# Which engine computes the low halves of two weight units behind the output projection

## The chip, the cores and the metric

The kernel runs on one core of one Trainium2 chip. The metric is the device time of one launch in microseconds (us), the median of several runs. Five engines work side by side, each through its own queue in order: TensorE (PE in the profile, PEld for its weight loads), VectorE (DVE), ScalarE (ACT), GpSimd (POOL) and SyncE (SP), which here only issues transfers.

## What is computed

The reference is one step of a two-layer decoder trunk, run for a prompt of 512 tokens and for 64 sample tokens (8 sequences of 8) with the same weights. One layer, cut to what matters here:

```python
h    = x * (1 + sc1) + sh1
proj = h @ w_in                                  # 22 blocks of 128 columns
mix  = concat([retention(proj), sliding_window(proj)]) @ w_out      # 8 blocks
x    = layer_norm(ALPHA * x + g1 * mix, ln1_g, ln1_b)
h2   = x * (1 + sc2) + sh2
up   = h2 @ w_up                                 # 44 blocks
f    = silu(conv3(up)_a) * conv3(up)_b
x    = layer_norm(ALPHA * x + g2 * (f @ w_down), ln2_g, ln2_b)      # 22 units
```

## The kernel before, in words

Everything lies transposed: 128 features on the partitions, 576 tokens along a row, so `x` is eight tiles of 128x576. Tokens are worked on in two halves of 288 (`HA`).

**Weights.** All weights come as a stream of units of 128x1024 f32, 96 for a layer (`UNITS`): 22 for `w_in`, 8 for `w_out`, 44 for `w_up`, 22 for `w_down`, in order of use. `Weights` (lines 72 to 113) keeps the stream running two units ahead of the one being multiplied. For each unit `u` a transfer on SP's queue brings the raw unit into one of two buffers `wr` (line 81). `_emit` then makes two operands: ScalarE casts the raw unit to `wh` (line 90), and one of two engines writes the rest that the cast lost, `wl = wr - wh` (line 95). This subtraction is called the split below. `wh` and `wl` have four buffers each; a raw buffer is free again when both have been made. The product of one tile of weights and one tile of activations is three matmuls, high by high, high by low, low by high, so a block of 128 columns and one half of the tokens is 24 matmuls (`gemm`, line 448).

**Which engine splits** is a rule on the unit's number in its layer, `v` (lines 92 to 94): GpSimd takes those marked `early`, and every third one that isn't `late`; VectorE takes the others. Units 30 to 33 of each layer are the first four of `w_up`: the four units behind the output products. Before, all four are `early`.

**The stage around them.** The last four `w_out` blocks are multiplied for the first half of the tokens, then for the second (`out_half` at line 1133 in `halves` at 1076). Behind each block's product stands a chain on other engines: VectorE adds the gated product to the base (`add_gated`, lines 560 to 564), ScalarE squares it (531), VectorE adds the square to a running sum `sq` (532), and GpSimd adds the block to a running sum `sd`; for the last block, 7, VectorE does that add (`r_done`, line 529). `stats` (line 534) then multiplies `sd` and `sq` by a matrix of ones on TensorE (`pd`, `pq`), and a chain of ScalarE and VectorE steps makes the mean and the inverse deviation, normalises (553, 554) and makes the operands `hi`, `lo` of the next product (`make_h`, 284 to 290).

The first four blocks of `w_up` (`up_first`, line 1206, through `skewed`, 1063) run for the first half of the tokens, for which the norm is ready, while the norm of the second half is still in work; then for the second half. So TensorE has 4 x 24 matmuls with which to cover the second half's sums, statistics and norm, and the matmuls of `stats(1)` stand somewhere among them in its queue. The same shape stands between the layers, with `w_down` in place of `w_out` and the next layer's first four `w_in` units in place of the four of `w_up`.

**What sets the order.** Each engine's queue is fixed when the kernel is built: a planner plays the traced program with its own estimates of durations and gives an idle engine the ready instruction that was traced first. Where an instruction is traced thus sets its priority, and its place in the queue can be before older ones that the planner did not yet hold for ready. On the chip the queue is kept to, whatever is ready.

Of the kernel before, what the change touches and what calls it, by code (L numbers as in the profile page):

```python
# [29 lines left out]
N_IN, N_OUT, N_UP, N_DN = 22, 8, 44, 22  # L30
UNITS = N_IN + N_OUT + N_UP + N_DN
# [40 lines left out]
class Weights:  # L72
# [10 lines left out]
    def _emit(self, u):  # L83
        nc, pool = self.nc, self.pool
        if u not in self.raw:
            self.load(u)
        raw = self.raw.pop(u)
        hi = pool.tile([P, 1024], F32R, tag="wh", name=f"wh{u}", bufs=4)
        lo = pool.tile([P, 1024], F32R, tag="wl", name=f"wl{u}", bufs=4)
        cast = nc.scalar.copy(hi, raw)  # L90
        v = u % UNITS
        late = v >= UNITS - 5 or N_IN + 3 <= v < N_IN + N_OUT
        early = v < 3 or N_IN + N_OUT <= v < N_IN + N_OUT + 4
        eng = nc.gpsimd if (early and u != 2) or (v % 3 == 2 and not late and u != 2) else nc.vector
        sub = eng.tensor_tensor(lo, raw, hi.bitcast(F32), ALU.subtract)  # L95
        if u in (2, 3):
            self.tc.keep_in_program_order(cast)
            self.tc.keep_in_program_order(sub)
        self.units[u] = (hi, lo)
# [1362 lines left out]
```

## Time and profile before

| | us |
|---|---|
| median of 3 runs | 1491.98 (1489.99 to 1494.51) |
| the profiled execution | 1492.97 |
| span of its trace | 1491.1 |
| around the span (the difference) | 1.87 |
| TensorE busy | 1447.6 (97%) |
| VectorE busy | 836.4 (56%) |
| ScalarE busy | 628.1 (42%) |
| GpSimd busy | 477.6 (32%) |

A row of the timeline gives the start and the length in us, the engine, the line, the operation, the tile written and those read, and in brackets how long the engine had been idle and who ended that. `x2` joins two neighbours of one kind in a row. A matmul's length overlaps that of its neighbours, so distances between starts count. The granted clock is a share of TensorE's full 2.4 GHz; its other level is 1.2 GHz. Names carry the layer (`l0`, `l1`), then the tile: `l0up1h` is the product of `w_up` block 1, `l0asd` the sum `sd` of layer 0's first norm, `l0a1pd` the statistics of its second half, `l0bsd` and `l0b1pd` those of its second norm.

### The profile page before, as it was taken

To read this page: it belongs to the slowest core of one execution; us is meant where nothing else is said; L and a number is where in the kernel's file an instruction comes from. 1 tells how busy PE (TensorE), PEld (TensorE's weight loads), DVE (VectorE), ACT (ScalarE), POOL (GpSimd) and SP (SyncE) were. 2 spreads that over 40 slices of the span, in tenths; PEclk is the share of its full clock that TensorE was granted. 3 is DMA by queue.
4 is the path that set the end of the run, shared out by engine and by line. 5 is a ranking of instruction groups with operands and counts; after the bars stand their busy time and mean duration, and the time that the engine had idled before them with its cause. 6 is when DMAs were issued, how large, how long until landed. Compare 5 with 4: busy or idle time off the path is not lost.

```text
span 1491.1 us, 28188 instructions
## 1 busy us (share of the span) xinstructions
PE 1447.6 (97%) x11248; PEld 1359.3 (91%) x11248; DVE 836.4 (56%) x1710; ACT 628.1 (42%) x1282; POOL 477.6 (32%) x646
## 2 busy tenths in 40 slices
PE   6999999999999999999999999999999999999996
PEld 3878889989989999999999889899899999999996
DVE  3257467657654255435566776666675435544565
ACT  2333323348542144325447342334765325523544
POOL 2122212363422132213373312207443213312353
PEclk8999999999999999999999999999999999999999
DMA  9586743333364645332224433332232222222221
GB/s 347 176 262 199 231 140 113 99 123 99 98 225 157 231 157 194 104 90 91 83 71 134 118 94 107 97 98 85 75 100 89 85 81 81 83 86 88 85 61 64
DMA packets 98191, 186.49 MB, mean 125 GB/s; under 512 B 30301, under 2 KB 42765, under 8 KB 97933
## 3 DMA queue, kind: packets, MB, share of 16 engines
q1 hardware_dynamic: 82768, 176.65, 37.6%
q10 hardware_dynamic: 15292, 8.06, 1.9%
q8 instruction: 88, 1.44, 0.4%
q14 instruction: 43, 0.34, 0.1%
HBM read 169.69 MB, written 11.83 MB: 122 GB/s over the span
## 4 chain that ended last, share of the span: by engine, by line
PE 88%; DVE 3%; DMA 3%; ACT 2%; issue 2%; POOL 1%; SPq 0%; ACTq 0%; POOLq 0%; DVEq 0%
PE ada L134 3%; PE l1wo L134 2%; PE l0wo L134 2%; PE l1wdl L134 1%; PE l0wdl L134 1%; DMA wr<-in_wst 1%; PE l1o L134 1%; PE l0o L134 1%; DMA wa<-in_w_ada 1%; POOL wl L95 1%; DMA bias_rows<-bias_row 1%; PE l0kv L134 1%; DVE wl L95 1%; PE l1up2h L134 0%; PE l0up2h L134 0%
## 5 line engine op out<-in xcount | busy, mean ns | idle before, releaser
L90 ACT CAST wh<-wr 128x1024 fp32r<-128x1024 f32 x192 | 200.7, 1048 | 320.1 <-DMA wr<-in_wst 20.1
L95 POOL TENSOR_TENSOR wl<-wr,wh 128x1024 fp32r<-128x1024 f32 x65 | 157.6, 2424 | 433.2 <-ACT wh L90 380.6
L95 DVE TENSOR_TENSOR wl<-wr,wh 128x1024 fp32r<-128x1024 f32 x127 | 160.2, 1262 | 169.8 <-ACT wh L90 151.3
L1172 POOL COPY l0edge<-l0u 128x2 f32<-128x2 f32 x44 | 37.5, 853 | 126.2 <-ACT l0u L1166 126.2
L1180 DVE SCALAR_TENSOR_TENSOR l0c<-l0u,par,l0c 128x592 f32<-128x592 f32 x44 | 48.2, 1098 | 47.2 <-ACT l0c L1179 44.3
L1172 POOL COPY l1edge<-l1u 128x2 f32<-128x2 f32 x44 | 37.6, 854 | 112.7 <-ACT l1u L1166 112.7
L1180 DVE SCALAR_TENSOR_TENSOR l1c<-l1u,par,l1c 128x592 f32<-128x592 f32 x44 | 48.5, 1104 | 44.1 <-ACT l1c L1179 41.3
L134 PE MATMUL ada<-wa,cs 128*32 128x512 f32 (+1 forms) x416 | 58.6, 582 | 5.2 <-DVE cs L184 5.2
L134 PEld LDWEIGHTS ada<-wa,cs 128*32 128x32 f32 x416 | 14.8, 112 | 32.0 <-issue 16.4
L1179 ACT ACTIVATE l1c<-l1u,par 128x592 f32<-128x592 f32 x44 | 38.9, 887 | 3.3
L1179 ACT ACTIVATE l0c<-l0u,par 128x592 f32<-128x592 f32 x44 | 38.9, 887 | 3.3
L1181 DVE SCALAR_TENSOR_TENSOR l1c<-l1u,par,l1c 128x592 f32<-128x592 f32 x44 | 36.6, 834 | 1.4
L1181 DVE SCALAR_TENSOR_TENSOR l0c<-l0u,par,l0c 128x592 f32<-128x592 f32 x44 | 36.6, 834 | 1.4
L481 ACT CAST l0fhi<-l0c 128x512 fp32r<-128x512 f32 (+1 forms) x44 | 16.8, 430 | 46.3 <-DVE l0c L1186 46.3
L481 ACT CAST l1fhi<-l1c 128x512 fp32r<-128x512 f32 (+1 forms) x44 | 16.9, 430 | 37.6 <-DVE l1c L1186 37.6
L796 POOL TENSOR_TENSOR l0sw<-l0sw,c_sin 128x576 f32<-128x576 f32 x8 | 14.3, 1783 | 38.6 <-DMA l0sw<-l0raw 38.6
L796 POOL TENSOR_TENSOR l1sw<-l1sw,c_sin 128x576 f32<-128x576 f32 x8 | 13.0, 1622 | 40.0 <-DMA l1sw<-l1raw 40.0
L482 DVE TENSOR_TENSOR l1flo<-l1c,l1fhi 128x512 fp32r<-128x512 f32 (+1 forms) x44 | 18.2, 454 | 13.0 <-ACT l1fhi L481 13.0
L482 DVE TENSOR_TENSOR l0flo<-l0c,l0fhi 128x512 fp32r<-128x512 f32 (+1 forms) x44 | 18.2, 454 | 12.4 <-ACT l0fhi L481 12.4
L1185 ACT ACTIVATE l1c<-l1c 128x592 f32<-128x592 f32 x22 | 15.4, 698 | 15.0 <-DVE l1c L1181 15.0
L504 POOL TENSOR_TENSOR l1xb<-l1xb,l1ash 128x288 f32<-128x288 f32 x12 | 12.7, 1086 | 25.9 <-issue 25.9
L504 POOL TENSOR_TENSOR l0xb<-l0xb,l0ash 128x288 f32<-128x288 f32 x12 | 12.7, 1087 | 25.9 <-issue 25.9
(3246 smaller groups left out, 5849.0 us busy)
## 6 DMA issues: line engine op xcount, KB each, us to landing
wr<-in_wst SPq DMA_DIRECT2D x192, 512.0 KB, 3.6
wa<-in_w_ada SPq DMA_DIRECT2D x192, 256.0 KB, 5.0
x<-in_xT SPq DMA_DIRECT2D x8, 288.0 KB, 6.2
l0sw<-l0raw SPq DMA_DIRECT2D x32, 72.0 KB, 2.7
l0xb<-in_xT SPq DMA_DIRECT2D x8, 288.0 KB, 3.3
x_spill<-l0x ACTq DMA_DIRECT2D x8, 288.0 KB, 3.2
l1sw<-l1raw SPq DMA_DIRECT2D x32, 72.0 KB, 2.1
l1xb<-x_spill SPq DMA_DIRECT2D x8, 288.0 KB, 3.1
```

Source lines behind the costliest of these rows:

```text
L90: cast = nc.scalar.copy(hi, raw)
L95: sub = eng.tensor_tensor(lo, raw, hi.bitcast(F32), ALU.subtract)
L134: self._add(nc.tensor.matmul(*args, **kw))
L481: S.copy(hi, src)
L482: V.tensor_tensor(lo, src, hi.bitcast(F32), ALU.subtract)
L504: G.tensor_tensor(base[:, o], base[:, o], self.shift[:, o], ALU.subtract)
L796: G.tensor_tensor(sw, sw, sin_t, ALU.mult)
L1172: G.tensor_copy(cm[:, 0:2], t[:, 512:514])
L1179: S.activation(c, t[:, 0:592], AF.Identity, bias=w[3], scale=w[0])
L1180: V.scalar_tensor_tensor(c, t[:, 1:593], w[1], c, ALU.mult, ALU.add)
L1181: V.scalar_tensor_tensor(c, t[:, 2:594], w[2], c, ALU.mult, ALU.add)
L1185: S.activation(ca, ca, AF.Silu)
```

## The change

Units 32 and 33 of each layer leave the set `early` and enter the set `late`, so their splits are issued on VectorE instead of GpSimd. `late` is needed for 32, which is one of the every-third units; 33 would go to VectorE without it. Units 30 and 31 stay on GpSimd. Casts, transfers, buffers and products are as before.

```diff
         v = u % UNITS
-        late = v >= UNITS - 5 or N_IN + 3 <= v < N_IN + N_OUT
-        early = v < 3 or N_IN + N_OUT <= v < N_IN + N_OUT + 4
+        late = v >= UNITS - 5 or N_IN + 3 <= v < N_IN + N_OUT or N_IN + N_OUT + 2 <= v < N_IN + N_OUT + 4
+        early = v < 3 or N_IN + N_OUT <= v < N_IN + N_OUT + 2
         eng = nc.gpsimd if (early and u != 2) or (v % 3 == 2 and not late and u != 2) else nc.vector
         sub = eng.tensor_tensor(lo, raw, hi.bitcast(F32), ALU.subtract)
```

## Rows read from the trace of the kernel before

**Rows 1.** The page: each engine's busy time, share of the span, and instructions.

```profile
PE 1447.6 (97%) x11248; PEld 1359.3 (91%) x11248; DVE 836.4 (56%) x1710; ACT 628.1 (42%) x1282; POOL 477.6 (32%) x646
```

**Rows 2.** TensorE's waits over the span: us in total, times, longest.

```profile
PE l0a1pd L134 <- DVE l0asd L529: 3.5, 1, 3.5
PE l1a1pd L134 <- DVE l1asd L529: 3.5, 1, 3.5
```

**Rows 3.** Timeline of TensorE, layer 0, from the first to the fifth block of w_up.

```profile
326.00 0.37 PE L134 MATMUL l0up0h<-l0ghi,wh 128*128 128x288 f32 x1
...
334.98 1.33 PE L134 MATMUL l0a1pd<-l0asd,ones_f 128*128 128x288 f32 x2 [3.48 <-DVE l0asd L529]
...
346.05 0.30 PE L134 MATMUL l0up0h<-l0ghi,wh 128*128 128x288 f32 x1
...
359.06 0.29 PE L134 MATMUL l0up4a<-l0ghi,wh 128*128 128x288 f32 x1
```

**Rows 4.** Timeline of VectorE, layer 0, second half: the adds and sums of the last blocks.

```profile
329.19 0.21 DVE L564 TENSOR_TENSOR l0x<-l0wo,l0xb 128x64 f32<-128x64 f32 x1
...
329.58 0.23 DVE L564 TENSOR_TENSOR l0x<-l0wo,l0xb 128x64 f32<-128x64 f32 x1
330.45 0.46 DVE L532 TENSOR_TENSOR l0asq<-l0a1s,l0asq 128x288 f32<-128x288 f32 x1 [0.65 <-ACT l0a1s L531]
334.47 0.46 DVE L529 TENSOR_TENSOR l0asd<-l0asd,l0x 128x288 f32<-128x288 f32 x1 [3.56 <-POOL l0asd L529]
```

**Rows 5.** Timeline of GpSimd in the same stretch: splits of units 32, 33, last sum.

```profile
328.21 2.41 POOL L95 TENSOR_TENSOR wl<-wr,wh 128x1024 fp32r<-128x1024 f32 x1 [1.46 <-ACT wh L90]
...
331.33 2.35 POOL L95 TENSOR_TENSOR wl<-wr,wh 128x1024 fp32r<-128x1024 f32 x1
333.63 0.81 POOL L529 TENSOR_TENSOR l0asd<-l0asd,l0x 128x288 f32<-128x288 f32 x1
```

**Rows 6.** Timeline of ScalarE: casts of units 32, 33, and of 34, 35.

```profile
327.07 1.06 ACT L90 CAST wh<-wr 128x1024 fp32r<-128x1024 f32 x1
...
328.64 1.06 ACT L90 CAST wh<-wr 128x1024 fp32r<-128x1024 f32 x1
...
353.56 2.02 ACT L90 CAST wh<-wr 128x1024 fp32r<-128x1024 f32 x2
```

**Rows 7.** Stretches: length, busy us by engine (PE, PEld, DVE, ACT, POOL), granted clock, DMA.

```profile
335.00:341.00 6.00, 6.00 (x22) 5.43 (x23) 3.92 (x7) 2.04 (x5) 2.48 (x5) 0.53 0.60 200
...
1056.00:1061.00 5.00, 5.00 (x23) 4.79 (x24) 3.97 (x8) 2.04 (x5) 2.51 (x5) 0.66 0.25 102
```

**Rows 8.** Timeline of TensorE, layer 1, from the first to the fifth block.

```profile
1046.98 0.37 PE L134 MATMUL l1up0h<-l1ghi,wh 128*128 128x288 f32 x1
...
1078.96 0.29 PE L134 MATMUL l1up4a<-l1ghi,wh 128*128 128x288 f32 x1
```

**Rows 9.** Timeline of TensorE between the layers, from the first to the fifth block.

```profile
782.92 0.37 PE L134 MATMUL l1kv0h<-l0nhi,wh 128*128 128x288 f32 x1 [1.06 <-DVE l0x L564]
...
789.66 0.68 PE L134 MATMUL l0b1pd<-l0bsd,ones_f 128*128 128x288 f32 x2
...
797.46 0.40 PE L134 MATMUL l1kv0h<-l0nhi,wh 128*128 128x288 f32 x1 [0.59 <-ACT l0nhi L289]
...
811.33 0.29 PE L134 MATMUL l1r01a<-l0nhi,wh 128*128 128x288 f32 x1
```

**Rows 10.** Timeline between the layers: a split on VectorE, then a sum on GpSimd.

```profile
787.16 1.22 DVE L95 TENSOR_TENSOR wl<-wr,wh 128x1024 fp32r<-128x1024 f32 x1
...
787.54 1.49 POOL L529 TENSOR_TENSOR l0bsd<-l0bsd,l0x 128x288 f32<-128x288 f32 x1 [0.64 <-DVE l0wdl L563]
```

**Rows 11.** All splits: count, shortest/median/longest ns, first and last start in us.

```profile
L95 DVE TENSOR_TENSOR wl<-wr,wh x127: 1210/1226/2307, 48.8 to 1452.1; 128x1024 fp32r<-128x1024 f32 x127
L95 POOL TENSOR_TENSOR wl<-wr,wh x65: 2333/2402/2877, 18.5 to 1410.9; 128x1024 fp32r<-128x1024 f32 x65
```

**Rows 12.** The chain that ended last: a block's 24 matmuls in steady running.

```profile
362.38 3.19 PE l0up4b L134 x24
```

## The prediction

> **What bounds the kernel now.** I read the busy times first, then TensorE's waits over the whole span, then the timelines of the stage that the change touches, and last the same stage elsewhere. TensorE is busy 97% of the span, VectorE 56%, GpSimd 32% [rows 1]. So an edit on VectorE or GpSimd is worth only what it takes from a wait of TensorE, or puts into one. Among those waits two stand out, one in each layer, of the same 3.5 us and the same cause: the statistics matmul of the first norm's second half waits for VectorE's last add into the running sum `sd` [rows 2]. Both lie in the stage behind the output products, where units 32 and 33 are split.
>
> The queues say why. In layer 0 blocks 6 and 7 of the second half are complete at 329.40 and 329.81 (starts 329.19 and 329.58 and their lengths) [rows 4]. The sum needs one GpSimd add for block 6, then VectorE's for block 7. But GpSimd holds the split of unit 32 from 328.21 and that of unit 33 from 331.33 to 333.68; only then comes the add of block 6, at 333.63 [rows 5]. VectorE, idle for 3.56 us, adds block 7 at 334.47 [rows 4], and the statistics start at 334.98, TensorE having been idle 3.48 us [rows 3]. The reader is to see that both splits, of 2.41 and 2.35 us, stand ahead of an add of 0.81 us for which three engines wait.
>
> The second cost is the clock. Behind the wait it is 0.53 of full speed for the 6 us from 335, and in layer 1 0.66 for 5 us [rows 7]: much of each stretch ran at 1.2 instead of 2.4 GHz. TensorE had been idle 3.48 us before either. Between the layers, where the same statistics meet no wait, the same pair of matmuls takes 0.68 us instead of 1.33 [rows 3, 9].
>
> **What the change removes.** Four of the 192 splits move (units 32 and 33 of two layers). GpSimd loses 2 x 2.4 us in each layer, and its add of block 6 can start when the block is there, 329.40, and end 0.81 later at 330.21; VectorE's add of 0.46 would end near 330.7. That is 4.2 us before the 334.93 of now, more than the wait, so the 3.48 us can go whole, if what is added does not come in its place.
>
> Worked out part by part, what is at stake in layer 0 is the wait, 3.48, and the clock, 6.00 x (1 - 0.53) = 2.8; together 6.3. In layer 1 it is 3.48 + 5.00 x (1 - 0.66) = 5.2. Whole stages say the same: from the first matmul of `w_up` block 0 to the first of block 4 it is 359.06 - 326.00 = 33.06 us in layer 0 [rows 3] and 1078.96 - 1046.98 = 31.98 in layer 1 [rows 8]. The matmuls in it are 8 groups of 24 at 3.19 [rows 12], 25.5 us, and two pairs of statistics at 0.68 [rows 9], 26.9 in all. So the excess is 6.2 and 5.1, nearly all of it those two terms.
>
> **What it adds.** Two splits of 1.23 us a layer on VectorE (median of the 127 there; 2.40 on GpSimd) [rows 11]. Their casts end at 328.13 and 329.70 [rows 6], so they become ready in the middle of VectorE's work on blocks 5 to 7, and where the planner puts them in VectorE's queue is not to be seen in this trace. I bound it from both sides. At best they stand behind the add of block 7 or in spots where VectorE idles anyway, such as the 0.65 us before 330.45 [rows 4]: cost 0 on the chain. At worst short of a blocked queue both stand ahead of that add: 2 x 1.23 = 2.46 us. The row nearest to this is the stage between the layers, where one such split does stand on VectorE in the middle of the same adds, at 787.16 [rows 10], and GpSimd's add that began meanwhile, at 787.54, took 1.49 us instead of 0.81 [rows 5, 10]. So a split also costs 0.68 where it meets an add on GpSimd.
>
> The Trainium skill speaks against the change here: "SBUF — State Buffer", section "Who interferes with whom", has VectorE instructions with two SBUF inputs and GpSimd instructions that read SBUF exclude each other, whichever starts second being held until the other ends. The stretched add agrees: the split ended at 788.38, and a wait until then and 0.81 make 789.19, against 789.03 measured. By that rule alone the sum below would lose another 0.68 a layer, 1.4 us, if the second split meets an add as well.
>
> **What comes late next.** When the wait is gone, the second half's norm sets the pace: between the layers TensorE reaches the second half 797.46 - 789.66 = 7.8 us after the statistics, and waits there 0.59 for the first `hi` [rows 9]. In layer 0 that distance is 346.05 - 334.98 = 11.1 [rows 3], long because slow matmuls and their copies stood between. So part of the gain is given back to the norm's chain. Rather than guess how much, I take the stage between the layers whole: 811.33 - 782.92 = 28.41 us [rows 9] for the same 192 matmuls and two statistics, with one split on VectorE, one stretched add, and full clock behind them. It has 1.5 us of excess over the 26.9.
>
> At no cost: the products of units 32 and 33 come after blocks 0 and 1, behind the statistics even now, and a VectorE split lasts half as long, so `wl` is not late. The raw buffers come free at another moment, but the next casts from them are at 353.56 [rows 6], 20 us later. No transfer is moved; SP's and GpSimd's queues lose nothing but the splits. If that cover of 20 us were gone, a late load would show as a wait of the cast for `wr`.
>
> **Sum.** 33.06 - 28.41 = 4.65 in layer 0, 31.98 - 28.41 = 3.57 in layer 1: 8.2 us. Everything behind runs at TensorE's pace and moves up. Against the profiled execution (span 1491.1 and 1.87 around it) 1492.97 - 8.2 = 1484.8; the median of the runs shown is 0.99 below that execution, so 1483.8, rounded to 1484.0. The bounds: no excess left in either stage, 6.2 + 5.1 = 11.3, gives 1480.7; a second split of 1.23 and its meeting of 0.68 on the chain of each layer leaves 8.2 - 3.8 = 4.4, 1487.6.
>
> **The rivals.**
> *The splits take the place of the wait* (chance 0.24). Both stand ahead of the add of block 7, so it ends at 330.7 + 2.46 = 333.2 instead of 334.93, or at 334.5 with two meetings of 0.68. The statistics come 0.4 to 1.8 us sooner; the clock gives back nothing to all of 2.8 and 1.7. Over both layers 0.8 to 8.1 us, in the middle 4: about 1488. For it: the splits are ready just there, and between the layers the planner did put one ahead. Against it: that one cost TensorE no wait at the statistics.
>
> *VectorE is blocked by a cast* (0.07), the slower one. The planner holds a cast for ready sooner than the chip does: GpSimd waited 1.46 us for unit 32's [rows 5]. If both splits stand on VectorE ahead of blocks 6 and 7, each costs up to 1.46 + 1.23 = 2.7 us, and everything of the adds and of `lo` is queued behind them. Block 7 then ends 5.4 us later, at 335.2, its add near 336.1: 1.2 us later than now in each layer, and with as much again for a longer slow stretch some 5 us: 1497. It decides from the point at which a split stands ahead of the adds of block 6 (329.19).
>
> *It comes to nothing* (0.07): splits stay where they were, or the norm's chain was as late anyway and TensorE waits at the second half instead. Against the first: by the rule of lines 92 to 94 units 32 and 33 fall to VectorE whatever else holds. Against the second stand the 7.8 us between the layers. About 1492.
>
> **How the numbers follow.** The forecast, 4.5 to 11 us gained, 0.62; the rivals 0.24, 0.07 and 0.07. A difference of 0.3%, 4.5 us, is about what a measurement of this kernel tells from none. Faster by that: 0.62 and some 0.09 of the first rival, 0.71. Within it: the other 0.15, the third rival and a little of the second, 0.23. Slower: 0.06. The range reaches from the bound of no excess, 1480.7, less the spread of the runs, to 1490.5, which takes in nearly all of the first rival and leaves out the other two.
>
> **What would show it.** Right: in the changed kernel's profile VectorE has 131 splits and GpSimd 61; the two 3.5 us rows are gone from TensorE's waits or under 1 us; the clock is 1.00 behind the statistics; GpSimd's last `sd` add starts within 1 us of block 6; both stages are 27 to 30 us long, with new waits under 1.5 us for `hi` or `lo` at the second half. Wrong: a split on VectorE between the add of block 6 and that of block 7 with a wait of over 1.5 us still on the statistics (first rival); VectorE idle for `wh` in front of a split at that place (second); or a planner's new order that loses time in stages which the change does not touch, which no row here can bound.

## The result, and the profile after

| | before | after |
|---|---|---|
| median, us | 1492.09 (1489.06 to 1495.45, 7 runs) | 1483.85 (1482.85 to 1487.35, 7 runs) |
| ratio | | 0.9945, 95% interval 0.9933 to 0.9958 |
| span of the profiled execution, us | 1491.1 | 1482.1 |

The kernel is 8.2 us faster, 0.55%. The mean granted clock of one execution lay between 0.985 and 0.992 over eighteen executions of the kernel before, and the time went with it, from 1497.05 to 1485.74 us; over the seven of the changed kernel it was 0.990 to 0.992. The page of the changed kernel gives each engine's busy time, which answers to [rows 1]:

```profile
PE 1442.0 (97%) x11248; PEld 1352.8 (91%) x11248; DVE 845.8 (57%) x1714; ACT 627.7 (42%) x1282; POOL 472.7 (32%) x642
```

All splits of the changed kernel (engine, count, shortest/median/longest ns, first and last start) answer to [rows 11]:

```profile
L95 DVE TENSOR_TENSOR wl<-wr,wh x131: 1211/1226/2426, 50.1 to 1443.0; 128x1024 fp32r<-128x1024 f32 x131
L95 POOL TENSOR_TENSOR wl<-wr,wh x61: 2339/2402/2772, 18.7 to 1401.8; 128x1024 fp32r<-128x1024 f32 x61
```

Four splits have changed engines, and VectorE is busy 9.4 us longer, in a kernel that is 8.2 us shorter: busy shares say nothing here. TensorE's waits do. In the two stages behind the output products the changed kernel has one wait each, where [rows 2] had the statistics' 3.5 us:

```profile
PE l0up0h L134 <- ACT l0ghi L289: 1.5, 1, 1.5
PE l1up0h L134 <- ACT l1ghi L289: 1.5, 1, 1.5
```

The timeline of TensorE in layer 0 answers to [rows 3]. Its rows are the start of the stage, the statistics, the start of the second half and the fifth block:

```profile
323.37 0.37 PE L134 MATMUL l0up0h<-l0ghi,wh 128*128 128x288 f32 x1
...
330.69 0.65 PE L134 MATMUL l0a1pd<-l0asd,ones_f 128*128 128x288 f32 x2
...
338.76 0.40 PE L134 MATMUL l0up0h<-l0ghi,wh 128*128 128x288 f32 x1 [1.54 <-ACT l0ghi L289]
...
351.95 0.29 PE L134 MATMUL l0up4a<-l0ghi,wh 128*128 128x288 f32 x1
```

The statistics meet no wait, the pair takes 0.65 us where it took 1.33 [rows 3], and the stage lasts 351.95 - 323.37 = 28.58 us. The stretches of six microseconds from the stage's start (length, then busy us of PE, PEld, DVE, ACT, POOL, then granted clock, DMA share and GB/s) answer to [rows 7]:

```profile
323.30:329.30 6.00, 6.00 (x46) 5.96 (x46) 5.79 (x16) 4.90 (x11) 4.00 (x5) 1.00 0.86 316
329.30:335.30 6.00, 6.00 (x44) 5.79 (x44) 4.59 (x9) 2.22 (x6) 3.42 (x8) 1.00 0.79 253
335.30:341.30 6.00, 4.46 (x32) 4.01 (x31) 5.78 (x22) 5.17 (x13) 2.32 (x3) 1.00 0.29 89
```

The clock is full throughout. So far this is the forecast. The queues of VectorE and GpSimd aren't. Their timeline in layer 0, from the end of block 6 of the second half (first row) on; the POOL row is GpSimd's last add into the sum:

```profile
326.55 0.21 DVE L564 TENSOR_TENSOR l0x<-l0wo,l0xb 128x64 f32<-128x64 f32 x1
...
326.81 1.22 DVE L95 TENSOR_TENSOR wl<-wr,wh 128x1024 fp32r<-128x1024 f32 x1
326.91 1.79 POOL L529 TENSOR_TENSOR l0asd<-l0asd,l0x 128x288 f32<-128x288 f32 x1 [0.73 <-DVE l0wo L563]
...
327.95 0.45 DVE L532 TENSOR_TENSOR l0asq<-l0a1s,l0asq 128x288 f32<-128x288 f32 x1
...
328.45 1.34 DVE L95 TENSOR_TENSOR wl<-wr,wh 128x1024 fp32r<-128x1024 f32 x1
329.71 0.45 DVE L529 TENSOR_TENSOR l0asd<-l0asd,l0x 128x288 f32<-128x288 f32 x1
```

Both splits stand ahead of block 7's add (329.71), and block 6's add on GpSimd, begun 0.10 us after the first split, took 1.79 us instead of 0.81. The sum is ready 329.71 + 0.45 - 323.37 = 6.8 us after the stage's start. In before it was (334.47 + 0.46 - 326.00) 8.9 [rows 3, 4]. That is 2.1 us sooner, not the 4.2 of the prediction.

Why then is there no wait? The planner moved the statistics in TensorE's queue as well: they stood behind 40 matmuls of the stage before, and now stand behind 55. The trace shows it: 55 matmuls at 3.19/24 = 0.133 us [rows 12] are 7.3 us, and the statistics start at 330.69 - 323.37 = 7.32, when the sum has been ready for half a microsecond. So two things changed at once, the sum's time and the statistics' place. Most experiments serve to tell them apart.

One table holds the stages of all kernels, in us from the first matmul of `w_up` block 0; each is a distance between starts of two rows of TensorE's timeline. "Second half" is where block 0 is multiplied for the second half of the tokens; the stage ends at block 4. The waits are TensorE's at the statistics and at the start of the second half, for its first `hi` or, in gbehind, its first `lo`.

| kernel | layer | statistics at | second half at | stage | waits |
|---|---|---|---|---|---|
| before | 0 | 8.98 | 20.05 | 33.06 | 3.48, none |
| before | 1 | 8.98 | 18.97 | 31.98 | 3.48, none |
| after | 0 and 1 | 7.32 | 15.39 | 28.58, 28.56 | none, 1.54 |
| place55 | 0 and 1 | 9.02 | 16.90 | 29.89, 29.90 | 1.67, 1.11 |
| after40 | 0 | 6.84 | 15.42 | 28.45 | 1.37, none |
| only32 | 0 | 8.02 | 15.90 | 28.88 | 1.60, 0.19 |
| only33 | 0 | 7.76 | 15.65 | 28.63 | 1.34, 0.20 |
| behind | 0 and 1 | 4.90 | 15.10 | 28.08, 28.07 | none, 1.01 |
| gbehind | 0 and 1 | 5.28 | 14.39 | 27.93, 27.93 | 0.44, 0.43 |
| all4 | 0 | 7.33 | 15.40 | 28.57 | none, 1.54 |
| all4 | 1 | 8.66 | 16.73 | 29.91 | none, 1.54 |

The stages account for the result: 33.06 - 28.58 = 4.48 in layer 0 and 31.98 - 28.56 = 3.42 in layer 1, 7.9 of the 8.2 us. The two spans differ by 9.0: in the profiled execution of after the stage of layer 0 also began 2.63 us earlier, and 1.45 us were lost again between its end and the stage of layer 1 (689.37 us against 687.92). Neither is the change: a second profile of the same changed kernel has the start at 326.95, against 323.37 here and 326.00 in before, and 687.65 us between the stages. The stage between the layers is untouched, 28.40 us against 28.41 [rows 9].

The table also tells how much of the gain is wait and how much is clock. A stage less its own waits is 27.02 to 27.11 us in every stage whose clock was 1.00: 28.58 - 1.54 = 27.04 in after, 29.89 - 1.67 - 1.11 = 27.11 in place55, 27.93 - 0.44 - 0.43 = 27.06 in gbehind. In before it is 33.06 - 3.48 = 29.58 and 31.98 - 3.48 = 28.50, so the slow stretches cost about 2.5 and 1.4 us there. Of after's 4.48 and 3.42 us, then, 3.48 - 1.54 = 1.94 in each layer is wait, and the other 2.5 and 1.5 is clock.

### The profile page after: what moved, and what is told of

The parts are those of the page before. It is cut to its first block, busy times and chain, and to the rows that moved or that the text cites. A ratio compares the mean times of both kernels' runs of the same rounds, so it can differ in the third digit from the quotient of the medians.

```text
span 1482.1 us, 28189 instructions
## 1 busy us (share of the span) xinstructions
PE 1442.0 (97%) x11248; PEld 1352.8 (91%) x11248; DVE 845.8 (57%) x1714; ACT 627.7 (42%) x1282; POOL 472.7 (32%) x642
## 4 chain that ended last, share of the span: by engine, by line
PE 84%; DVE 3%; ACT 2%; issue 1%; DMA 1%; SPq 0%; POOL 0%; ACTq 0%; POOLq 0%; DVEq 0%
PE ada L134 2%; PE l0wo L134 2%; PE l1wo L134 2%; PE l1wdl L134 2%; PE l0wdl L134 1%; PE l1o L134 1%; PE l0o L134 1%; PE l1up0h L134 0%; PE l0up0h L134 0%; PE l1av L134 0%; PE l1kv0h L134 0%; ACT y L1290 0%; PE l1up3h L134 0%; PE l0up3h L134 0%; PE l0up2h L134 0%
## 5 line engine op out<-in xcount | busy, mean ns | idle before, releaser
L95 POOL TENSOR_TENSOR wl<-wr,wh 128x1024 fp32r<-128x1024 f32 x61 | 147.5, 2419 | 422.7 <-ACT wh L90 370.3
L95 DVE TENSOR_TENSOR wl<-wr,wh 128x1024 fp32r<-128x1024 f32 x131 | 165.2, 1262 | 166.4 <-ACT wh L90 147.7
L234 DVE TENSOR_TENSOR mod<-adat,par 128x36 f32<-128x36 f32 (+1 forms) x26 | 3.8, 185 | 31.6 <-PE adat L137 31.6
L1157 POOL COPY l0u<-l0edge 128x16 f32<-128x16 f32 x44 | 21.6, 503 | 0.0
```

The lines of the kernel that those rows point to most:

```text
L1157: G.tensor_copy(t[:, 514:594].rearrange("p (b t) -> p b t", b=8)[:, :, 0:2], hist[mt // 11][:, mt % 11, :].rearrange("p (b t) -> p b t", b=8))
```

## The experiments

### The place of the statistics alone

The kernel before, with the statistics traced in `w_up` block 2 after six of its matmuls, so that they stand behind 54 matmuls, near where the change puts them. All splits stay on GpSimd.

```diff
-    def gemm(tiles, X, out, half, between=None):
+    def gemm(tiles, X, out, half, between=None, at=2):
...
-            if between and k == n - 2:
+            if between and k == n - at:
...
-    def skewed(items, between):
+    def skewed(items, between, at=0, left=0):
...
-                gemm(tiles(), hcur[0], ps, half)
+                mid = left > 0 and half == 0 and n == at
+                gemm(tiles(), hcur[0], ps, half, between if mid else None, left)
...
-            skewed([it_up(mt) for mt in range(4)], lambda: (ln.stats(1), norm_h(1, st2, "g")))
+            skewed([it_up(mt) for mt in range(4)], lambda: (ln.stats(1), norm_h(1, st2, "g")), 2, 6)
```

> GpSimd keeps all four splits, as before; only the statistics of the second half are traced later, so that they stand in TensorE's queue behind 54 of the first half's matmuls (before: 40, changed kernel: 55). The sums are ready 9.0 us after the stage's first matmul, as before. Theory 'chain' (the second half starts some 8 us after the statistics, the statistics start when the sums are there): TensorE reaches them at 7.2 us, waits 1.8, second half at 9.0 + 8.1 = 17.1, stages 30.3 us instead of 33.06 and 31.98, a gain of 4.4, about 1487.5. Rival 'place alone' (the changed kernel won because its statistics stand later in the queue): stages as in the changed kernel, 28.6 us, about 1484. Rival 'sums alone' (only the time at which the sums are ready counts, the place nothing): no gain, about 1492.

Measured: 1488.41 us, ratio 0.9974 (0.9960 to 0.9989). TensorE's timeline shows the wait cut in two:

```profile
335.60 0.75 PE L134 MATMUL l0a1pd<-l0asd,ones_f 128*128 128x288 f32 x2 [1.67 <-DVE l0asd L529]
...
343.48 0.40 PE L134 MATMUL l0up0h<-l0ghi,wh 128*128 128x288 f32 x1 [1.11 <-ACT l0ghi L289]
```

The stretches of the same kernel, in the same columns as before:

```profile
332.00:338.00 6.00, 4.33 (x30) 3.88 (x29) 1.88 (x5) 1.64 (x4) 4.43 (x8) 1.00 0.64 224
338.00:344.00 6.00, 4.88 (x38) 4.65 (x37) 6.00 (x15) 3.53 (x8) 3.85 (x5) 1.00 0.29 99
```

The statistics start when they did, 9.02 us into the stage against 8.98. But after a wait of 1.67 us the clock stayed at 1.00, and the second half followed 7.9 us behind the statistics, where before it took 11.1 and 10.0. The stages fell by 33.06 - 29.89 = 3.2 and 31.98 - 29.90 = 2.1 us with no sum a moment sooner. Only 3.48 - 1.67 - 1.11 = 0.70 us of that is wait; the other 2.5 and 1.4 us are the slow stretch that is gone. The stage is near the 30.3 us of the theory 'chain'. The rival 'place alone' wanted 28.6, and 'sums alone' no gain; neither came.

### The sooner sums with the old place

The changed kernel with the same edit of `gemm` and `skewed`, and with the first half's matmuls kept in the traced order, so that the statistics stand behind 39 of them.

```diff
...
+            T.pinned = left > 0 and half == 0
...
-            skewed([it_up(mt) for mt in range(4)], lambda: (ln.stats(1), norm_h(1, st2, "g")))
+            skewed([it_up(mt) for mt in range(4)], lambda: (ln.stats(1), norm_h(1, st2, "g")), 1, 3)
```

> The changed kernel's splits, but TensorE's queue of the first half is kept as traced, with the statistics behind 39 matmuls, where the kernel before had them (40). Theory 'chain': TensorE reaches the statistics at 5.6 us and waits 1.6 for the sums, the second half starts at 7.3 + 8.1 = 15.4 us as in the changed kernel, where it waited 1.54 just there; the wait only moves forward, stages 28.6 us (30 if the clock falls behind the wait), 1484 to 1487. Rival 'place alone': the place of before brings back its wait, stages 30.3 us or more, 1488 or more. Rival 'sums alone': 1484.

Measured: 1485.0 us, ratio 0.9952 (0.9933 to 0.9971), stage 28.45. TensorE waits at the statistics again, but briefly:

```profile
329.32 0.75 PE L134 MATMUL l0a1pd<-l0asd,ones_f 128*128 128x288 f32 x2 [1.37 <-DVE l0asd L529]
```

The stretches around and behind it, in the columns of before:

```profile
326.00:332.00 6.00, 4.63 (x32) 4.18 (x32) 4.97 (x11) 2.67 (x8) 4.58 (x9) 1.00 0.84 261
332.00:338.00 6.00, 6.00 (x48) 6.00 (x47) 5.65 (x14) 3.64 (x9) 3.64 (x5) 1.00 0.39 133
```

The clock stays full, and a wait of 1.37 us at the statistics merely takes the place of the 1.54 at the second half. With sums this early the place is worth nothing, and 'place alone', which wanted 30.3 us or more, is out. So the two effects do not add: either of them alone removes the long wait. Between place55 and after the sooner sums are worth 29.89 - 28.58 = 1.3 us a layer, and that is the difference of the waits, 1.67 + 1.11 - 1.54 = 1.24; the rest of the gain is that no slow stretch follows.

### One split at a time

Only unit 32 goes to VectorE, then only unit 33; the other stays on GpSimd. In both kernels the statistics stand behind 47 matmuls, so their place moves here too.

```diff
-        late = v >= UNITS - 5 or N_IN + 3 <= v < N_IN + N_OUT
-        early = v < 3 or N_IN + N_OUT <= v < N_IN + N_OUT + 4
+        late = v >= UNITS - 5 or N_IN + 3 <= v < N_IN + N_OUT or v == N_IN + N_OUT + 2
+        early = v < 3 or (N_IN + N_OUT <= v < N_IN + N_OUT + 4 and v != N_IN + N_OUT + 2)
```

> Only unit 32 moves to VectorE, 33 stays on GpSimd. The queues as built: GpSimd has its three adds ahead of the split of 33, VectorE one split ahead of block 7's add, statistics behind 47 matmuls. Theory 'chain': sums ready at about 6.2 us, statistics at 6.3, second half at 14.4, stages 27.7 us, about 1482, some 2 us better than the changed kernel. Rival 'each split is worth half': a gain of 4.1, about 1488.

Measured: 1485.53 us, ratio 0.9953 (0.9934 to 0.9972), stage 28.88: missed. GpSimd's split of unit 33 and VectorE's add of block 7, in the timeline, show why:

```profile
330.51 2.37 POOL L95 TENSOR_TENSOR wl<-wr,wh 128x1024 fp32r<-128x1024 f32 x1
...
330.59 2.61 DVE L529 TENSOR_TENSOR l0asd<-l0asd,l0x 128x288 f32<-128x288 f32 x1 [0.20 <-POOL l0asd L529]
```

The queue of VectorE was free and the add was issued in time, 0.08 us behind the start of GpSimd's split. It then took 2.61 us instead of 0.45: it ended 0.32 us after the split. The expectation had put that split behind the sums and so at no cost; it cost the sum 2.2 us from the other engine. The Trainium skill ("SBUF — State Buffer", section "Who interferes with whom") says just this of a VectorE instruction with two SBUF inputs and a GpSimd one that reads SBUF, whichever starts second. The trace agrees: held until the split's end at 332.88 and then 0.45 us long, the add would end at 333.33, against 333.20 measured. The prediction had weighed only the side on which GpSimd is held.

The other one, unit 33 alone:

```diff
-        early = v < 3 or N_IN + N_OUT <= v < N_IN + N_OUT + 4
+        early = v < 3 or N_IN + N_OUT <= v < N_IN + N_OUT + 3
```

> Only unit 33 moves to VectorE, 32 stays on GpSimd. GpSimd has the split of 32 ahead of the adds of blocks 5 and 6, VectorE the split of 33 ahead of block 7's add, statistics behind 47 matmuls. Theory 'chain': the split of 32 ends 4.6 us after the stage's start, adds at 5.4 and 6.2 (7.2 if VectorE's split stretches one), sums ready at 6.7 to 7.7, TensorE waits 0.5 to 1.4, second half at 15 to 16 us, stages 28.5 to 29.3, 1484 to 1486. Rival 'each split is worth half': 1488.

Measured: 1484.84 us, ratio 0.9946 (0.9927 to 0.9965), stage 28.63, as expected. GpSimd's split of unit 32, VectorE's split and GpSimd's two last adds in the timeline:

```profile
328.20 2.41 POOL L95 TENSOR_TENSOR wl<-wr,wh 128x1024 fp32r<-128x1024 f32 x1 [1.45 <-ACT wh L90]
...
329.73 1.96 DVE L95 TENSOR_TENSOR wl<-wr,wh 128x1024 fp32r<-128x1024 f32 x1 [0.19 <-ACT wh L90]
...
330.57 2.66 POOL L529 TENSOR_TENSOR l0asd<-l0asd,l0x 128x288 f32<-128x288 f32 x2
```

VectorE's split began while GpSimd's still ran and is stretched from 1.23 to 1.96 us; the two adds began while VectorE's split ran and are stretched from 1.62 to 2.66. Moving one split gives all but 0.1 to 0.3 us a layer of what moving both gives: already one of them makes the wait short (1.60, 1.34).

### Splits behind the sums

If what counts is what stands ahead of the sums, then the splits should go behind them, on either engine. On VectorE first: the changed kernel, with units 32 and 33 issued behind the second half's last add into `sq` (line 532).

```diff
-            V.tensor_tensor(self.sq[:, o], t, self.sq[:, o], ALU.add)
+            self.end = V.tensor_tensor(self.sq[:, o], t, self.sq[:, o], ALU.add)
...
+            with tc.issue_after(ln.end.ins):
+                W.upto(nf + 3)
```

> The changed kernel, with the two VectorE splits (units 32 and 33) issued behind the last of the second half's sums instead of ahead of block 7's add; the statistics then stand behind 36 matmuls of block 0 in TensorE's queue (55 in the changed kernel). Theory 'order' (each microsecond by which the sums come sooner comes back in the stage as long as no wait is long enough to slow the clock): the sums are ready some 5.3 us after the stage's start instead of 7.3, the statistics start at about +5.3, the splits take 2.45 us after them on VectorE and delay the norm's next VectorE step by about 1.2 us, so the second half starts near +14.35 and the stage takes 27.4 to 28.0 us against 28.57: about 1482 us, 1 to 2 us better than the changed kernel. Rival 'the order of splits and sums does not matter, only which engine splits': stages of 28.6 us, 1484.

Measured: 1484.37 us, ratio 0.9947 (0.9930 to 0.9964), stage 28.08. The sum came sooner than expected, the second half didn't. VectorE behind the sums:

```profile
329.96 2.96 DVE L95 TENSOR_TENSOR wl<-wr,wh 128x1024 fp32r<-128x1024 f32 x2
332.85 0.44 DVE L543 TENSOR_TENSOR l0a1var<-l0a1pq,l0a1var 128x288 f32<-128x288 f32 x1
```

The norm's first VectorE step (line 543) follows the start of the statistics by 332.85 - 329.17 = 3.7 us; in after, by 331.93 - 330.69 = 1.2. The splits had only moved from ahead of the sums to between them and the norm: the statistics started 2.4 us sooner, the second half 0.3. The expectation had this delay at 1.2 and it was 2.4, two whole splits. The stage is 0.5 us shorter than after's; the medians can't tell that apart.

Then on GpSimd: the kernel before with its engines for all four units, block 7's add of the second half moved to GpSimd too, and the two splits issued behind it. (Lines from 530 on count one more in this kernel.)

```diff
-                (V if m == 7 else G).tensor_tensor(self.sd[:, o], self.sd[:, o], x[:, o], ALU.add)
+                own = m == 7 and not (half and nm[2] == "a")
+                self.end = (V if own else G).tensor_tensor(self.sd[:, o], self.sd[:, o], x[:, o], ALU.add)
...
+            with tc.issue_after(ln.end.ins):
+                W.upto(nf + 3)
```

> The kernel before, with all four splits of units 30 to 33 still on GpSimd, but the last two issued behind the second half's sums, and block 7's add of the second half on GpSimd, in front of them; the statistics stand behind 35 matmuls of block 0. Theory 'order' (the gain of the change is that the sums no longer queue behind splits, whichever engine splits): sums at about +5.0 us, statistics at +5.3, second half near +13.2 to +13.8 (TensorE's own matmuls end there), stage 26.9 to 27.5 us, about 1481 us; GpSimd's two splits end near +7.4 and +9.8, when TensorE reaches the units at about +7.5 and +10.7, so waits on them stay under 1 us. Rival 'the engine' (GpSimd is too slow for these two units): waits of 1 to 3 us for the units' low halves or a stage as long as before's, 32 to 33 us, 1488 or more.

Measured: 1482.98 us, ratio 0.9935 (0.9919 to 0.9951), stage 27.93. GpSimd's adds and splits in the timeline:

```profile
328.07 1.68 POOL L530 TENSOR_TENSOR l0asd<-l0asd,l0x 128x288 f32<-128x288 f32 x2 [0.73 <-DVE l0wo L564]
329.72 4.74 POOL L95 TENSOR_TENSOR wl<-wr,wh 128x1024 fp32r<-128x1024 f32 x2
```

TensorE's waits in that stage:

```profile
PE l0a1pd L134 <- POOL l0asd L530: 0.4, 1, 0.4
PE l0up0h L134 <- DVE l0glo L290: 0.4, 1, 0.4
```

GpSimd makes the same four splits as before, at the same 2.4 us each, and TensorE waits for none of them. The sum is ready 5.2 us into the stage. The statistics stand behind 35 matmuls, fewer than before, so their place has no part in it. The gain of the change is to be had without its change of engine: it came from what stood ahead of the sums. (The run also moves block 7's add to GpSimd; what that is worth by itself was not measured.) The stage missed the upper end of its 26.9 to 27.5 us by 0.4; its two waits are 0.9 together.

### All four units on VectorE

The changed kernel, with units 30 and 31 split by VectorE too.

```diff
-        late = v >= UNITS - 5 or N_IN + 3 <= v < N_IN + N_OUT or N_IN + N_OUT + 2 <= v < N_IN + N_OUT + 4
-        early = v < 3 or N_IN + N_OUT <= v < N_IN + N_OUT + 2
+        late = v >= UNITS - 5 or N_IN + 3 <= v < N_IN + N_OUT or v == N_IN + N_OUT + 2
+        early = v < 3
```

> The changed kernel, with units 30 and 31 split by VectorE too (all four, 30 to 33). The two added splits stand in VectorE's queue between the steps of the first half's norm, ahead of the stage measured so far. Theory 'chain' (a split costs its time wherever it stands in a chain that TensorE waits for, and nothing elsewhere): 1.2 to 2.5 us a layer come back before the stage, which itself stays at 28.5 us: 1486 to 1489. Rival 'VectorE is the better engine for these units anywhere': 1484 or less.

Measured: 1492.39 us, ratio 0.9996 (0.9984 to 1.0007): the whole gain is gone, more than expected. The timeline of TensorE at the start of the two stages has waits that after hasn't:

```profile
327.06 0.37 PE L134 MATMUL l0up0h<-l0ghi,wh 128*128 128x288 f32 x1 [2.26 <-DVE l0x L564]
...
1049.51 0.58 PE L134 MATMUL l1up0h<-l1ghi,wh 128*128 128x288 f32 x1 [2.80 <-DVE l1wo L563]
```

The two splits of layer 1 on VectorE, in the first half's norm, and a GpSimd step of that norm between their starts:

```profile
1039.38 1.21 DVE L95 TENSOR_TENSOR wl<-wr,wh 128x1024 fp32r<-128x1024 f32 x1
...
1040.05 1.98 POOL L554 TENSOR_TENSOR l1x<-l1x,l1ars 128x288 f32<-128x288 f32 x2 [1.76 <-ACT l1ars L547]
...
1041.30 1.81 DVE L95 TENSOR_TENSOR wl<-wr,wh 128x1024 fp32r<-128x1024 f32 x1
```

And the stretches behind the two waits:

```profile
327.00:333.00 6.00, 5.93 (x45) 5.97 (x46) 5.79 (x16) 3.93 (x10) 4.01 (x5) 1.00 0.40 109
...
1049.00:1055.00 6.00, 5.49 (x31) 5.52 (x32) 5.29 (x14) 3.56 (x10) 3.85 (x9) 0.72 0.07 19
```

The splits stand in a chain that TensorE waits for, at 1.21 + 1.81 = 3.0 us instead of 2.46. Behind the 2.80 us of layer 1 the clock fell to 0.72, which makes that stage 29.91 - 28.56 = 1.35 longer. Together 2.26 + 2.80 + 1.35 = 6.4 us. By the ratios the loss against after is about 0.0051 x 1492 = 7.6; the rest isn't traced. VectorE is not the better engine for these units as such.

### The change and the GpSimd version side by side

> The changed kernel as it is, once more, beside the version with GpSimd's splits behind the sums, on one chip. Both theories (order of the queue, engine of the split) expect 1483 to 1485 us of it, and a stage of 28.6 us.

> The version that leaves all four splits on GpSimd and issues the last two behind the sums (gbehind), once more. Theory 'order': its stages are 0.64 us shorter than the changed kernel's, so it is some 1.3 us (0.09%) faster than the changed kernel on the same chip, 1482 to 1483.5 us. Rival 'the engine': it is slower than the changed kernel.

Measured on one chip: the change 1484.85 us (1480.67 to 1486.2), ratio 0.9950 (0.9931 to 0.9969); the GpSimd version 1482.31 us (1481.42 to 1485.24), ratio 0.9934 (0.9911 to 0.9956). Stages 28.55 and 28.57 against 27.92 and 27.92, as the first time. In both pairs of medians the GpSimd version is ahead, by 0.9 us (not on one chip) and 2.5; the runs overlap, and what is firm is 0.64 us a layer in the traces.

## Why the prediction was right, and where it was not

- **The bound** was right: the two waits of 3.48 us and the slow clock behind them were what an edit there could take. Both are gone, with a wait of 1.54 us at the second half in their place. The clock, put at 2.8 and 1.7 us, gave back 2.5 and 1.5.
- **The sum** was right: 8.2 us forecast, 8.2 measured, 7.9 of it in the two stages. Taking the stage between the layers whole, 28.41 us, was the step that carried it: the stages came out at 28.58 and 28.56. That they agree to 0.2 us is in part luck. Between the layers the second half begins after 797.46 - 782.92 = 14.54 us and lasts 811.33 - 797.46 = 13.87 [rows 9]; here it begins 0.85 us later, after 15.39, and lasts 0.68 us less, 351.95 - 338.76 = 13.19. The second half follows the statistics by 338.76 - 330.69 = 8.07 us, nearly as there (7.8), but the wait in front of it is 1.54 where it was 0.59 there.
- **The removed part** was mis-sized. The prediction let block 6's add take 0.81 us and the sum come 4.2 us sooner; the add took 1.79 and the sum came 2.1 us sooner. The meeting with a VectorE split, priced at 0.68, cost 0.98.
- **The place of the splits** was left open, between 0 and 2.46 us; they took the worst of it, both ahead of block 7's add. That is the first rival's placement. It put the add of block 7 at 0.4 to 1.8 us sooner; it ended 2.1 sooner. Its bounds of 0.8 to 8.1 us for both layers take in the 7.9, so the number alone doesn't tell the forecast from this rival; its middle, about 1488, was off. It let the clock give back nothing to all, in the middle half; in the traces of the changed kernel the clock of these stages never fell. In two runs a wait of 1.67 us (place55) or 1.37 (after40) was followed by no slow stretch either, so there a sum 2 us sooner was as good for this term as one 4 us sooner. That no such wait can slow the clock is not shown (last section).
- **Not foreseen:** the planner's new place for the statistics, behind 55 matmuls. after40 shows that the time doesn't hang on it, 28.45 us without it, 28.58 with it; place55 shows that it alone would have been worth 3.2 and 2.1 us.
- **The second rival** did not come: VectorE had no idle time in front of either split.
- **By its own list:** 131 and 61 splits, the two long waits gone, clock 1.00, GpSimd's last add 0.15 us after block 6 (complete at 326.55 + 0.21 = 326.76), stages of 27 to 30 us all came; the new wait of 1.54 is just over its 1.5. The sign for "wrong", a split between the adds of blocks 6 and 7, came as well, without its wait.

So the number was right for the right bound and by a well-chosen stage to compare with, though the inside of that stage was not as told, and two differences in it happened to cancel.

## What to carry to other kernels

When a long wait of TensorE is followed by a slow clock, look first at the slow stretch: cutting the 3.48 us to two waits of 1.67 and 1.11 gave back only 0.70 us of wait, but 2.5 and 1.4 us of clock, and all further gain in the sums was about 1.3. Before moving work to a faster engine, look whether the slow engine merely does it ahead of something urgent: put behind the urgent adds, the same splits on the slower engine made TensorE wait for none of them, and the kernel was no slower than with them on VectorE. And take a comparable stage of the same kernel whole, where there is one, rather than adding up guesses about a queue that isn't known yet.

## What the runs showed of the hardware that was not expected

- A VectorE subtraction or add of two SBUF tiles and a GpSimd operation that reads SBUF held each other off in both directions, for nearly all that was left of the one that began first: GpSimd's add took 1.79 us instead of 0.81 behind a VectorE split that had 1.12 to go, VectorE's add 2.61 instead of 0.45 behind a GpSimd split that had 2.29 to go, VectorE's split 1.81 and 1.96 instead of 1.23 behind GpSimd steps.
- In the stages measured here the granted clock stayed at 1.00 behind waits of 1.37, 1.67 and 2.26 us, and fell to 0.72 behind one of 2.80 and to 0.53 and 0.66 behind those of 3.48, counted over the 5 to 6 us that followed. Each of these is one stretch of one execution, and the length of the wait does not settle it. Early in layer 0 TensorE waits 1.83 us for a cast and, 1.3 us after that, 0.73 for a split, in after (at 67.24) and in place55 (at 66.75) alike. From 67 to 73 us the clock was 1.00 in after and 0.72 in place55. The stretch of 40 us around it, after first, then place55, shows the same:

```profile
60.00:100.00 40.00, 36.57 (x289) 31.50 (x289) 16.35 (x41) 12.84 (x34) 11.18 (x10) 1.00 0.80 264
60.00:100.00 40.00, 36.57 (x278) 31.51 (x277) 15.25 (x36) 11.87 (x31) 9.58 (x7) 0.96 0.75 248
```

What decided between them no run here shows.
